# Modulation sums in 1024-wide products, and spread softmax factors behind the value products

## The chip, the cores and the metric

The kernel runs on one core of one Trainium2 chip. The time is the device time of one execution in microseconds (us), as the median of the runs shown.

## What is computed

Two blocks run one after the other on 512 latent tokens of width 1024, with 256 context tokens beside them in the first block, all in float32.

The first block has two layers. Each makes twelve modulation vectors (six for the latent, six for the context) from a condition, projects the normed tokens, runs two attentions of 8 heads (one banded with a sink logit, one dense), merges them under gates, and ends in a gated FFN:

```python
mod   = silu(c) @ w_ada[l] + b_ada[l]          # 6 x 1024 numbers for the latent
mod_c = silu(c_ctx) @ w_ada[l] + b_ada[l]      # 6 x 1024 for the context
h  = rms_norm(x) * (1 + sc1) + sh1
qa, ka, va, qb, kb, vb, ga, gb = split(h @ w_in[l])
ya = window_attention(rope(qa), rope(ka), va, kac, vac, sink)   # p = softmax(s), y = p @ v
yb = full_attention(rope(norm(qb)), rope(norm(kb)), vb, kbc, vbc)
x = x + gt1 * ((sigmoid(ga) * (ya @ w_pa) + sigmoid(gb) * (yb @ w_pb)) @ w_o)
h2 = rms_norm(x) * (1 + sc2) + sh2
x = x + gt2 * swiglu(h2)
```

The second block has a mixer of three attention branches (compressed, selected, windowed), a gated linear recurrence, and a merge of the same form.

## The kernel before, in words

Tokens lie on the free axis and features on the partitions. Every matmul in float32 is three matmuls with both operands split into a high and a low part (`mm3`, L278 to 281). Weights stream through a ring: SyncE loads 128x1024 units (`w`), ScalarE casts the high part (`ws`, L167), GpSimd subtracts for the low part (L171). Each engine works through its own instructions in the order in which the program issues them; the program is one fixed order, written out by hand with hooks at chosen steps.

**Modulation.** Of layer 0 the first 16 weight tiles (shift and scale of the first norm) go through TensorE. The other 80 (`ADB`) are row tiles `wa` of 128x1024: `ada_rows` (L373) multiplies a tile with the broadcast condition `crs` on VectorE and sums along the free axis, for two conditions `c` and, before the change, in two halves of 512 (L382); the elementwise product goes to a tile `junk` that nobody reads. `ada_step` does a whole tile, `ada_half` one condition. `ada_load` issues the tile's load from ScalarE's queue into a ring of two buffers. Steps stand in the query-A projection (`project`, L894, for k = 2 to 7), the query-B projection (k = 0 to 4), the merge of layer 0 (L598, iterations 2 to 11, one condition each), the output projection (`out_proj`, as long as `ada_i < NADA0`) and the FFN of layer 0.

**Projections.** `project` runs over eight k; for each, hooks, then a step, then `mm3` for six token tiles into six PSUM banks (`zs`, `zt`). In query A the hooks carry the keys' work: transposes `ktp`, casts `kTh` on VectorE and ScalarE, low parts `kTl` on GpSimd (`k_parts`, L764 to 775). After it `q_evac` copies each bank to `q`, by turns on VectorE (L318) and ScalarE (L321), two token tiles in one `q` tile; query B's first matmuls reuse the banks.

**Attention.** `Attn.head` works through eight heads of a job (128 queries): scores `sc`, their maximum `nm` on VectorE, the exponential `pb` on ScalarE; three heads later `back` transposes `pb` (`tp`) and the copies go to `PT`. After head 7 `scales` makes the reciprocal sums and spreads them over 512 columns on VectorE (`two` or `Rs`, L1465). One head later `pv` runs: `spread` transposes these factors on TensorE (`Rb`, L1488, four transposes into a bank of the two-bank ring that `tp` uses too), ScalarE copies them back (L1489), the value products go to `pv` (L1477), and `y` multiplies both on VectorE (L1051; in the second block L1828 to 1831). For the last job of an attention (`flush`) the order was products first; for all others `spread` first. The compressed branch (`cmp_ops`, L1890) has its own products `cpv` and calls `spread` behind them. Between heads `Filler` pieces (`fil`) of the merge gates' matmuls are issued.

Of the kernel before, what the change touches and what calls it, by code (L numbers as in the profile page):

```python
# [11 lines left out]
F32 = mybir.dt.float32  # L12
F32R = mybir.dt.float32r
BF16 = mybir.dt.bfloat16
I32 = mybir.dt.int32
AF = mybir.ActivationFunctionType
ALU = mybir.AluOpType
# [4 lines left out]
P = 128  # L22
# [191 lines left out]
class Kern:  # L214
# [158 lines left out]
    def ada_rows(self, i, wt, cs=(0, 1)):  # L373

        V = self.V
        l, e = ADB[i]
        j = e % 4
        if j == 0 and 0 in cs:
            self.ada_sum = self.sm.tile([P, 2, 4, 2], F32, tag="adas", name="adas")
        for c in cs:  # L380
            for h in range(2):
                V.scalar_tensor_tensor(self.junk, wt[:, h * 512:(h + 1) * 512], 1.0, self.crs[:, c, h * 512:(h + 1) * 512],  # L382
                                       op0=ALU.mult, op1=ALU.mult, accum_out=self.ada_sum[:, h, j, c:c + 1])
        if j == 3 and 1 in cs:
            o = self.mods[l][:, e - 3:e + 1, :]
            V.tensor_tensor(o, self.ada_sum[:, 0], self.ada_sum[:, 1], op=ALU.add)
            V.tensor_tensor(o, o, self.C("b_ada", l * 48 + e - 3, 4)[:, :, None].to_broadcast([P, 4, 2]), op=ALU.add)
            self.ada_gain(l, e - 3, 4)

    def ada_open(self, first=False):  # L390

        kp = self.pool(self.right, "kp", 1, side="right")
        self.crs = kp.tile([P, 2, 1024], F32, name="crs")
        self.junk = None if first else kp.tile([P, 512], F32, name="junk")
        self.nc.sync.dma_start(self.crs, self.crow.to_broadcast([P, 2, 1024]))

    def ada_silu(self):
# [156 lines left out]
    def merge(self, pool, l, chunks, ya, yb, gd, nsg, fl):  # L554

        V, S, G, W = self.V, self.S, self.G, self.W
        order = [(n, t0, w) for n in range(8) for (t0, w) in chunks]
        sgs = {}

        def load(i):  # L560
            if i < len(order):
                n, t0, w = order[i]
                sg = pool.tile([P, 2, w], F32, tag=f"sg{w}", name="sg", bufs=nsg)
                for b in range(2):
                    self.nc.sync.dma_start(sg[:, b, :], gd[n][b][:, t0:t0 + w])
                sgs[i] = sg

        ahead = (nsg - 1) * len(chunks)
        for i in range(ahead):
            load(i)  # L570
        def sigmoid(i):
            if i < len(order):
                S.activation(sgs[i], sgs[i], AF.Sigmoid)

        fl.rest()
        low = None
        sigmoid(0)
        for i, (n, t0, w) in enumerate(order):
            if i % len(chunks) == 0:
                W.open(("mp", l, n))  # L580
            sigmoid(i + 1)
            sg = sgs.pop(i)
            for b, y in ((0, ya), (1, yb)) if l < 2 else ((1, yb), (0, ya)):
                pp = self.bank()
                parts = [y(k, t0, w) for k in range(4)]
                for j in range(len(parts[0])):
                    for k in range(4):
                        c0, cw, ab = parts[k][j]
                        self.mm3(pp[:, c0:c0 + cw], W.at(("mp", l, n), (b * 4 + k) * 128), ab, k == 0, k == 3)
                V.tensor_tensor(sg[:, b, :], sg[:, b, :], pp[:, :w], op=ALU.mult)  # L590
            if low:
                low()
            V.tensor_tensor(sg[:, 0, :], sg[:, 0, :], sg[:, 1, :], op=ALU.add)
            hi, lo = self.H(n, t0, w)
            S.copy(hi, sg[:, 0, :])
            if l == 0 and i == 1:
                self.ada_silu()
            elif l == 0 and 1 < i < 12:  # L598
                self.ada_half(i % 2)

            def low(i=i, hi=hi, lo=lo, sg=sg):
                V.tensor_tensor(lo, sg[:, 0, :], hi, op=ALU.subtract)
                load(i + ahead)

        low()
# [181 lines left out]
    def layer(self, l, hooks_in):  # L787
        V, S, G, T, W, C, sm = self.V, self.S, self.G, self.T, self.W, self.C, self.sm
# [88 lines left out]
        def project(c, tiles, free, hooks=()):  # L877
            hk = {}
            for at, fn in hooks:
                hk.setdefault(at, []).append(fn)  # L880
            z = {}
            for i in range(0, min(4, len(tiles)), 2):
                if len(tiles) - i >= 2 and tiles[i] < 4:
                    s = self.psS.tile([P, 2, 512], F32, tag="S", name="zs")
                    z[tiles[i]], z[tiles[i + 1]] = s[:, 0, :], s[:, 1, :]
            for t in tiles:
                if t not in z:
                    z[t] = self.psT.tile([P, 512], F32, tag="T", name="zt")
            for k in range(KD):
                for fn in hk.get(k, ()):  # L890
                    fn()
                if free:
                    W.open(("qkv", l, c), k * 512)
                if l == 0 and (c == "qb" and k < 5 or c == "qa" and k > 1):  # L894
                    self.ada_step(1 if c == "qb" and k == 4 else 2)
                for i, t in enumerate(tiles):
                    if i == len(tiles) // 2:
                        for fn in hk.get(k + 0.5, ()):
                            fn()
                    self.mm3(z[t], self.H(k, t * P, P), W.at(("qkv", l, c), k * 512, 512), k == 0, k == KD - 1)  # L900
            return z
# [25 lines left out]
        if l == 0:  # L927
            project0(hooks_in + [(9, tables)])
        else:
            z = project("kv", lat, False, hooks_in + [(7, tables)])  # L930
            for t in lat:
                kv_copy(t, z[t])
            z = project("kv", ctxt, True, [(2 * t, lambda t=t: kv_rest(t)) for t in lat])
            for t in ctxt:
                kv_copy(t, z[t])
# [10 lines left out]
        pq = self.pool(es, "pq", 1)  # L946
        at = Attn(self, pq, 3)
        if l == 0:
            self.junk = pq.tile([P, 512], F32, tag="qst", name="junk", bufs=2)

        def k_norm():
            self.rsq(rk.rearrange("p a b -> p (a b)"), ssk.rearrange("p a b -> p (a b)"), 12, 1.0 / HD, "kq")
# [51 lines left out]
        if l == 0:  # L1004
            khooks.append((1, self.ada_silu))
        z = project("qa", qt, True, [(0.5, k_norm)] + khooks)
        for t in qt:
            q_evac(0, t, z[t])
        first = dict(q=qs[0, 0])
# [326 lines left out]
class Attn:  # L1336
# [99 lines left out]
    def back(self):  # L1436
        K = self.K
        job, h, pb = self.pend.popleft()
        nb = job["nk"] // P
        for b0 in range(0, nb, 4):  # L1440
            m = min(4, nb - b0)
            tp = K.psT.tile([P, 4, P], F32, tag="T", name="tp")
            for i in range(m):
                K.T.transpose(tp[:, i, :], pb[:, (b0 + i) * P:(b0 + i + 1) * P], K.ident)  # L1444
            K.evac(self.PT[:, b0:b0 + m, h, :], tp[:, :m, :])
        if h == 7:
            rb = self.scales(job)
            self.tail.append((self.n + 1, lambda **kw: self.pv(job, rb, **kw)))

    def scales(self, job):  # L1450
        K = self.K
# [14 lines left out]
                      rs.rearrange("p (g j) -> p j g", g=2)[:, :, :, None].to_broadcast([P, 4, 2, HD]))  # L1466
        return rb

    def pv(self, job, rb, wait=False):
        K = self.K  # L1470
        pv = K.psV.tile([P, 512], F32, tag="V", name="pv")
        nb = job["nk"] // P
        if not wait:
            self.spread(job, rb)
        for b in range(nb):
            for g in range(2):
                K.T.matmul(pv[64 * g:64 * g + 64, :], job["v"](b)[:, 64 * g:64 * g + 64],  # L1477
                           self.PT[:, b, 4 * g:4 * g + 4, :], start=(b == 0), stop=(b == nb - 1))
        if wait:
            self.spread(job, rb)  # L1480
        job["y"](pv, job["Rs"])

    def spread(self, job, rb):
# [9 lines left out]
    def flush(self):  # L1493
        while self.pend:
            self.back()
        while self.tail:
            self.tail.popleft()[1](wait=True)


def second(K, nh):  # L1500
# [324 lines left out]
    def y(tb):  # L1825
        def f(pv, r):
            if parts[tb]:
                V.tensor_tensor(r, pv, r, op=ALU.mult)  # L1828
                V.tensor_tensor(yflat[tb], yflat[tb], r, op=ALU.add)
            else:  # L1830
                V.tensor_tensor(yflat[tb], pv, r, op=ALU.mult)
            parts[tb] += 1
            if parts[tb] == 3:
                V.tensor_tensor(yA[:, tb], yA[:, tb], ga[:, :, tb * P:(tb + 1) * P], op=ALU.mult)
        return f
# [296 lines left out]
```

## Time and profile before

| | |
|---|---|
| median of 3 runs | 2389.41 us (2389.12 to 2389.66) |
| profiled execution, own time | 2386.33 us |
| its span | 2384.30 us |
| mean granted clock of TensorE | 0.991 of full speed |
| TensorE matmuls busy | 97% of the span |
| VectorE busy | 57% |
| ScalarE busy | 37% |
| GpSimd busy | 33% |

The durations below are those of the profiled execution. In the profile PE is TensorE, PEld its weight loads, DVE is VectorE, ACT is ScalarE, POOL is GpSimd and SP is SyncE; L382 is line 382 of the kernel. An entry in square brackets at a row's end is the idle time of its engine ahead of it, and what ended it. Matmuls are pipelined: a duration of 0.39 us can go with starts 0.23 us apart.

### The profile page before, as it was taken

The numbers are of one execution on the slowest core, as the hardware profiler recorded it, in microseconds if no ns is written. First come the engines' busy times: TensorE is split into PE (matmuls) and PEld (weight loads), VectorE is DVE, ScalarE is ACT, GpSimd is POOL, SyncE is SP. The second block draws the span as 40 slices with busy tenths as digits, with TensorE's granted clock in tenths as the row PEclk, the third lists the DMA queues.
The fourth block names the chain that finished last, engine by engine and source line by source line (L and its number), as shares of the span: only waits on it lengthen the run. The fifth ranks groups of instructions, "written<-read, shape, count | busy, mean of one in ns | idle before, by whom it ended". The sixth has DMA issues, their size and how long they took to land.

```text
span 2384.3 us, 33287 instructions
## 1 busy us (share of the span) xinstructions
PE 2305.5 (97%) x13104; PEld 1902.5 (80%) x13104; DVE 1364.8 (57%) x2685; ACT 886.5 (37%) x1606; POOL 793.2 (33%) x367
## 2 busy tenths in 40 slices
PE   8799999999999999999999999999999999999999
PEld 7577787898888888888777777988888888776777
DVE  6976655578577686861685754461111168466552
ACT  4235455542321211122335555432222243464551
POOL 1621222231232333332262322524344433533232
PEclk9999999999999999999999999999999999999999
DMA  7431111363244343432121112513222323432143
GB/s 280 143 124 46 47 56 38 136 221 133 71 131 135 127 152 118 143 99 83 67 80 54 63 45 90 199 57 107 89 97 88 98 80 120 142 120 72 66 159 106
DMA packets 86404, 255.12 MB, mean 107 GB/s; under 512 B 9240, under 2 KB 16928, under 8 KB 85992
## 3 DMA queue, kind: packets, MB, share of 16 engines
q1 hardware_dynamic: 74664, 211.02, 26.1%
q10 hardware_dynamic: 11520, 41.95, 5.3%
q8 instruction: 103, 1.69, 0.3%
q14 instruction: 53, 0.43, 0.1%
q0 software_dynamic: 64, 0.02, 0.0%
HBM read 231.96 MB, written 23.61 MB: 107 GB/s over the span
## 4 chain that ended last, share of the span: by engine, by line
PE 78%; DVE 15%; ACT 3%; issue 2%; DMA 1%; POOL 0%; SPq 0%; ACTq 0%; DVEq 0%; POOLq 0%
PE gup L280 8%; PE gup L281 8%; PE gup L279 8%; PE pv L1477 4%; PE bt L279 4%; PE bt L280 4%; PE bt L281 4%; DVE junk L382 4%; PE tp L1444 4%; PE fil L279 3%; PE fil L281 3%; PE fil L280 3%; PE bs L279 3%; PE bs L281 3%; PE bs L280 3%
## 5 line engine op out<-in xcount | busy, mean ns | idle before, releaser
L171 POOL TENSOR_TENSOR ws<-w,ws 128x1024 fp32r<-128x1024 f32 x273 | 677.2, 2492 | 1313.1 <-ACT ws L167 1263.8
L167 ACT CAST ws<-w 128x1024 fp32r<-128x1024 f32 x274 | 281.0, 1044 | 253.2 <-PE bs L281 67.4
L382 DVE SCALAR_TENSOR_TENSOR junk<-wa,crs 128x512 f32<-128x512 f32 x320 | 344.6, 1077 | 10.8 <-DMA wa<-in_wada_dram 1.8
L280 PE MATMUL gup<-hl,ws 128*128 128x512 f32 (+1 forms) x736 | 284.0, 386 | 1.0 <-DVE hl L297 1.0
L279 PE MATMUL gup<-hl,ws 128*128 128x512 f32 (+1 forms) x736 | 283.6, 385 | 0.0
L281 PE MATMUL gup<-hl,ws 128*128 128x512 f32 (+1 forms) x736 | 283.4, 385 | 0.0
L671 DVE TENSOR_TENSOR g<-g,gup 128x512 f32<-128x512 f32 (+1 forms) x68 | 39.8, 585 | 334.0 <-ACT g L670 334.0
L670 ACT ACTIVATE g<-gup 128x512 f32<-128x512 f32 (+1 forms) x68 | 35.1, 516 | 402.6 <-PE gup L281 402.6
L1424 ACT ACTIVATE pb<-sc,nm 128x768 f32<-128x768 f32 (+3 forms) x160 | 120.5, 753 | 160.3 <-DVE nm L1421 75.4
L280 PEld LDWEIGHTS gup<-hl,ws 128*128 128x128 f32 x736 | 138.3, 188 | 31.6 <-DVE hl L297 2.1
L281 PEld LDWEIGHTS gup<-hl,ws 128*128 128x128 f32 x736 | 138.3, 188 | 30.1
L279 PEld LDWEIGHTS gup<-hl,ws 128*128 128x128 f32 x736 | 138.4, 188 | 29.2
L279 PE MATMUL fil<-hl,ws 128*128 128x512 f32 x384 | 154.6, 403 | 4.8 <-DVE gst L318 4.8
L281 PE MATMUL fil<-hl,ws 128*128 128x512 f32 x384 | 152.0, 396 | 0.1
L280 PE MATMUL fil<-hl,ws 128*128 128x512 f32 x384 | 151.7, 395 | 0.0
L1421 DVE TENSOR_REDUCE nm<-sc 128x1 f32<-128x768 f32 (+3 forms) x160 | 122.7, 767 | 47.5 <-PE sc L1410 46.6
L1444 PEld LDWEIGHTS tp<-cst,pb 128*128 128x128 f32 x896 | 105.8, 140 | 43.5 <-issue 20.1
L1444 PE MATMUL tp<-cst,pb 128*128 128x128 f32 x896 | 137.1, 275 | 3.2 <-ACT PT L321 1.3
L321 ACT COPY PT<-tp 128x512 f32<-128x512 f32 (+3 forms) x210 | 97.7, 476 | 85.7 <-PE tp L1444 85.5
L1376 POOL TENSOR_TENSOR qst<-two,qst 64x512 fp32r<-64x512 f32 x36 | 48.2, 1340 | 195.9 <-DVE qst L1375 189.6
L1409 PE MATMUL sc<-kTh,qst 128*128 128x256 f32 (+2 forms) x288 | 108.2, 376 | 4.3 <-ACT pb L1424 4.2
L279 PE MATMUL bt<-act,ws 128*128 128x512 f32 (+1 forms) x280 | 105.2, 376 | 1.2 <-DVE x L610 1.1
(438 smaller groups left out, 5619.8 us busy)
## 6 DMA issues: line engine op xcount, KB each, us to landing
w<-in_wts_dram SPq DMA_DIRECT2D x274, 512.0 KB, 3.3
wa<-in_wada_dram ACTq DMA_DIRECT2D x80, 512.0 KB, 3.4
gd<-gst SPq DMA_DIRECT2D x48, 256.0 KB, 2.0
sg<-gd SPq DMA_DIRECT2D x48, 256.0 KB, 4.0
wa<-in_wada_dram SPq DMA_DIRECT2D x16, 512.0 KB, 9.9
x<-in_xin_dram SPq DMA_DIRECT2D x8, 384.0 KB, 6.2
zd<-ud SPq DMA_DIRECT2D x1, 2560.0 KB
x<-in_xin_dram SPq DMA_DIRECT2D x4, 512.0 KB, 6.5
```

The lines of the kernel that those rows point to most:

```text
L167: nc.scalar.copy(s[:, 0, :], w)
L171: eng.tensor_tensor(s[:, 1, :], w, s[:, 0, :], op=ALU.subtract)
L279: T.matmul(out, a[0], b[0], start=first, stop=False)
L280: T.matmul(out, a[0], b[1], start=False, stop=False)
L281: T.matmul(out, a[1], b[0], start=False, stop=last)
L321: self.S.copy(dst, src)
L382: V.scalar_tensor_tensor(self.junk, wt[:, h * 512:(h + 1) * 512], 1.0, self.crs[:, c, h * 512:(h + 1) * 512], op0=ALU.mult, op1=ALU.mult, ...
L1409: T.matmul(ps[:, o:o + n], q, job["kh"](g)[:, c0:c0 + n], start=True, stop=False)
L1421: V.tensor_reduce(nm, sc, axis=AX.X, op=ALU.max, negate=True)
L1424: S.activation(pb[:, :nk], sc, AF.Exp, bias=nm, scale=sign, accum_out=job["sums"][:, h:h + 1])
L1444: K.T.transpose(tp[:, i, :], pb[:, (b0 + i) * P:(b0 + i + 1) * P], K.ident)
L1477: K.T.matmul(pv[64 * g:64 * g + 64, :], job["v"](b)[:, 64 * g:64 * g + 64], self.PT[:, b, 4 * g:4 * g + 4, :], start=(b == 0), stop=(b == ...
```

## The change

The sums take one product of 1024 per condition, and the addition of the two halves goes. `junk` is 1024 wide: in float32 where it shares a ring with the query tiles, and in bf16 in the tile that the merge and the FFN of layer 0 use. In the query-A projection steps stand at k = 2, 3 and 4 only; in the merge of layer 0 they go on to iteration 15; as the steps are taken in one sequence, the output projection takes one more (nine for eight). `pv` issues `spread` behind the value products in all jobs.

```diff
-            self.ada_sum = self.sm.tile([P, 2, 4, 2], F32, tag="adas", name="adas")
+            self.ada_sum = self.sm.tile([P, 4, 2], F32, tag="adas", name="adas")
         for c in cs:
-            for h in range(2):
-                V.scalar_tensor_tensor(self.junk, wt[:, h * 512:(h + 1) * 512], 1.0, self.crs[:, c, h * 512:(h + 1) * 512],
-                                       op0=ALU.mult, op1=ALU.mult, accum_out=self.ada_sum[:, h, j, c:c + 1])
+            V.scalar_tensor_tensor(self.junk, wt, 1.0, self.crs[:, c, :], op0=ALU.mult, op1=ALU.mult,
+                                   accum_out=self.ada_sum[:, j, c:c + 1])
         if j == 3 and 1 in cs:
-            o = self.mods[l][:, e - 3:e + 1, :]
-            V.tensor_tensor(o, self.ada_sum[:, 0], self.ada_sum[:, 1], op=ALU.add)
-            V.tensor_tensor(o, o, self.C("b_ada", l * 48 + e - 3, 4)[:, :, None].to_broadcast([P, 4, 2]), op=ALU.add)
+            V.tensor_tensor(self.mods[l][:, e - 3:e + 1, :], self.ada_sum,
+                            self.C("b_ada", l * 48 + e - 3, 4)[:, :, None].to_broadcast([P, 4, 2]), op=ALU.add)
...
-        self.junk = None if first else kp.tile([P, 512], F32, name="junk")
+        self.junk = None if first else kp.tile([P, 1024], BF16, name="junk")
...
-            elif l == 0 and 1 < i < 12:
+            elif l == 0 and i > 1:
                 self.ada_half(i % 2)
...
-                if l == 0 and (c == "qb" and k < 5 or c == "qa" and k > 1):
+                if l == 0 and (c == "qb" and k < 5 or c == "qa" and 1 < k < 5):
                     self.ada_step(1 if c == "qb" and k == 4 else 2)
...
-            self.junk = pq.tile([P, 512], F32, tag="qst", name="junk", bufs=2)
+            self.junk = pq.tile([P, 1024], F32, tag="qst", name="junk", bufs=2)
...
-    def pv(self, job, rb, wait=False):
+    def pv(self, job, rb):
...
-        if not wait:
-            self.spread(job, rb)
         for b in range(nb):
             for g in range(2):
                 K.T.matmul(pv[64 * g:64 * g + 64, :], job["v"](b)[:, 64 * g:64 * g + 64],
                            self.PT[:, b, 4 * g:4 * g + 4, :], start=(b == 0), stop=(b == nb - 1))
-        if wait:
-            self.spread(job, rb)
+        self.spread(job, rb)
         job["y"](pv, job["Rs"])
```

## Rows read from the trace of the kernel before

**Rows 1.** The page, busy time of each engine and share of the span.
```profile
PE 2305.5 (97%) x13104; PEld 1902.5 (80%) x13104; DVE 1364.8 (57%) x2685; ACT 886.5 (37%) x1606; POOL 793.2 (33%) x367
```
**Rows 2.** Waits of TensorE: waiting line, releaser, us in total, times, longest.
```profile
PE zs L279 <- ACT q L321: 17.1, 2, 16.7
PE Rb L1488 <- DVE two L1465: 6.8, 5, 2.5
PE Rb L1488 <- DVE Rs L1465: 1.8, 1, 1.8
```
**Rows 3.** Timeline of TensorE between query A and B: start, us, what.
```profile
104.87 0.39 PE L280 MATMUL zt<-ws,hc 128*128 128x512 f32 x1
105.10 0.40 PE L281 MATMUL zt<-ws,hc 128*128 128x512 f32 x1
122.16 0.79 PE L279 MATMUL zs<-ws,hl 128*128 128x512 f32 x1 [16.66 <-ACT q L321]
```
**Rows 4.** Timeline of VectorE and ScalarE in query A.
```profile
83.35 0.68 DVE L382 SCALAR_TENSOR_TENSOR junk<-wa,crs 128x512 f32<-128x512 f32 x1
...
84.07 1.67 DVE L382 SCALAR_TENSOR_TENSOR junk<-wa,crs 128x512 f32<-128x512 f32 x1
...
87.48 2.77 DVE L382 SCALAR_TENSOR_TENSOR junk<-wa,crs 128x512 f32<-128x512 f32 x1
...
96.13 1.11 DVE L382 SCALAR_TENSOR_TENSOR junk<-wa,crs 128x512 f32<-128x512 f32 x1
...
120.81 0.68 DVE L318 COPY q<-zs 128x512 f32<-128x512 f32 x1
121.52 0.58 ACT L321 COPY q<-zs 128x512 f32<-128x512 f32 x1 [11.43 <-DVE q L318]
```
**Rows 5.** Timeline of VectorE in the merge: a 1024-wide operation with two inputs.
```profile
459.36 1.21 DVE L285 TENSOR_TENSOR yl<-y,yh 128x1024 fp32r<-128x1024 f32 x1
```
**Rows 6.** The products alone in a window: length, VectorE busy, clock, DMA, GB/s.
```profile
83.00:120.85 37.85, 31.49 (x48) 0.83 0.33 111
```
**Rows 7.** Timeline of GpSimd in query A.
```profile
77.05 2.40 POOL L171 TENSOR_TENSOR ws<-w,ws 128x1024 fp32r<-128x1024 f32 x1 [6.73 <-ACT ws L167]
83.51 3.38 POOL L774 TENSOR_TENSOR kTl<-kraw,kTh 64x512 fp32r<-64x512 f32 x2 [4.05 <-DVE kTh L772]
```
**Rows 8.** Windows: length; PE, PEld, DVE, ACT, POOL busy; clock, DMA, GB/s.
```profile
122.10:125.20 3.10, 3.04 (x7) 2.46 (x8) 2.57 (x4) 2.03 (x4) 0.91 (x1) 0.51 0.53 169
518.00:532.00 14.00, 14.00 (x98) 12.94 (x97) 5.78 (x12) 7.03 (x10) 5.04 (x3) 1.00 0.48 163
```
**Rows 9.** Timeline of TensorE: three of the six factor transposes that waited.
```profile
191.75 0.63 PE L1488 MATMUL Rb<-cst,two 128*128 128x128 f32 x4 [2.27 <-DVE two L1465]
...
290.27 0.63 PE L1488 MATMUL Rb<-cst,two 128*128 128x128 f32 x4 [1.38 <-DVE two L1465]
...
1289.12 1.09 PE L1488 MATMUL Rb<-cst,two 128*128 128x128 f32 x4 [2.52 <-DVE two L1465]
```
**Rows 10.** Timeline: value products after two of these, and an evacuation ahead.
```profile
192.30 3.65 PE L1477 MATMUL pv<-PT,vt 128*64 128x512 f32 x16
...
1287.37 0.59 ACT L321 COPY PT<-tp 128x512 f32<-128x512 f32 x1
...
1290.14 4.80 PE L1477 MATMUL pv<-PT,vt 128*64 128x512 f32 x16
```
**Rows 11.** Timeline behind the compressed branch's products in the second block.
```profile
2144.21 0.66 PE L1488 MATMUL Rb<-cst,Rs 128*128 128x128 f32 x4
...
2145.54 0.66 PE L1361 MATMUL qtp<-cst,qtok 128*128 128x128 f32 x4 [0.39 <-ACT Rs L1489]
2145.57 0.69 DVE L1831 TENSOR_TENSOR yA<-cpv,Rs 128x512 f32<-128x512 f32 x1 [3.30 <-issue]
```
**Rows 12.** GpSimd's low parts of keys: count, duration ns min/median/max, starts, forms.
```profile
L774 POOL TENSOR_TENSOR kTl<-kraw,kTh x32: 716/1175/1737, 83.5 to 1239.7; 64x512 fp32r<-64x512 f32 x16, 64x256 fp32r<-64x256 f32 x16
L774 POOL TENSOR_TENSOR k2l<-kraw,k2h x8: 1264/1293/1455, 2046.9 to 2059.0; 64x512 fp32r<-64x512 f32 x8
```

More of the change, by code (lines that the diff above doesn't have):

```diff
@@ L1447, in back @@
             rb = self.scales(job)
-            self.tail.append((self.n + 1, lambda **kw: self.pv(job, rb, **kw)))
+            self.tail.append((self.n + 1, lambda: self.pv(job, rb)))
     def scales(self, job):
@@ L1496, in flush @@
         while self.tail:
-            self.tail.popleft()[1](wait=True)
+            self.tail.popleft()[1]()
 def second(K, nh):
```

## The prediction

> **What bounds the kernel now.** I read the page's engine totals first: TensorE is busy for 2305.5 of 2384.3 us [rows 1], so time can only come from its 79 us of idleness, or from matmuls at the low clock. Then the waits of TensorE, longest in total first: one wait of 16.7 us ends on a ScalarE copy of `q`, and six waits of 8.6 us together end on the softmax factors [rows 2]. No other row there reaches 7 us. The timeline around the long one shows where it lies: the last matmul of the query-A projection starts at 105.10, and the first of query B at 122.16 [rows 3]. The reader is to see that the ScalarE copy named as releaser is not the cause. VectorE's rows say what is: it makes the first copy of the projection's result at 120.81, 15 us after the result was there, because that copy stands in VectorE's own order behind 24 modulation products issued for k = 2 to 7; ScalarE's copy into the same `q` tile follows at 121.52 and TensorE starts 0.06 us after it ends [rows 3, 4]. So VectorE sets the time of this stage and TensorE that of all others.
>
> **Change, part 1: the products.** One weight tile and condition now cost one product of 1024 and one accumulator read instead of two of each. Undisturbed, a 512 product and its read take 0.72 us from start to start (83.35 to 84.07). A two-input VectorE operation of 1024 elements takes 1.21 us (`yl`); with the same 0.04 us between, I take 1.25 for the wide product [rows 4, 5]. The trace has no wide product with an accumulator and a bf16 output; bounds are 1.25 and 2 x 0.72 = 1.44.
>
> In query A, three steps stay (k = 2, 3, 4): 6 wide products for 24 narrow ones. From 83.35 to 120.81 VectorE needs 37.5 us; 31.5 of it are the products and reads [rows 4, 6]. Alone these would take 24 x 0.72 = 17.3. The other 6.0 us are casts, copies and small sums; one of the casts was stalled behind a weight subtraction, 2.1 by the price that follows, so own work is 17.3 + 3.9 = 21.2 and stalls are 16.3. The stalls have a pattern: a product that starts beside GpSimd's 64x512 subtractions takes 1.67 instead of 0.68 (+0.98), beside a 64x256 one 1.11 (+0.42), beside the 128x1024 weight subtraction 2.77 (+2.09) [rows 4, 7]. After the change own work is 6 x 1.25 + 3.5 = 11.0 (the small sums go with step four). GpSimd's queue is unchanged. Taking turns with it, the six products wait 0, 0.98, 2.09, 0.98, 0.42, 0.42 = 4.9; the seven casts of k behind the first, which mostly slipped through before, now meet GpSimd: four at 0.98, two at 0.42, one at 2.09 = 6.9. VectorE ends at 83.35 + 11.0 + 11.8 = 106.2 instead of 120.81. TensorE starts 1.35 us after that (120.81 to 122.16), at 107.5; its last matmul ends at 105.5 (105.10 + 0.40). A gap of 2.0 us stays, and of 16.7 **14.7 are gained**; I take 14.5, as the last copies round up.
>
> The clock: after the gap seven matmuls run at a granted clock of 0.51, the lower of its levels (1.2 GHz), and take 0.43 apart where 0.23 is usual, 1.4 us in all [rows 8]. Gaps of 2.3 and 2.5 us elsewhere were followed by the low clock in one case (1289.12) and not in the other (191.75) [rows 9, 10]. I count nothing, bounds 0 and 1.4 gained.
>
> **Part 2: where the steps go.** Merge iterations 12 to 15 take two of the three steps, four wide products of 1.25 = 5.0 us; the output projection takes the third. Each also brings its load of 512 KB, issued from ScalarE behind the cast of `hi`; that cast waits for a VectorE sum which stands behind the last use of the buffer, so the load finds it free, and in query A three load issues go that stood in ScalarE's order waiting for VectorE. Behind the products in VectorE's order stand the merge's own low halves, for which the output projection waits. From 518 to 532 VectorE is busy for 5.78 of 14 us while TensorE is busy for all 14 [rows 8]: 5.0 us fit, I take 0, and 5.0 if the cover were gone. Everywhere else in layer 0 (query B, merge, output projection, the first FFN) a step costs 2.5 us instead of 2.9; TensorE has no wait there that a product ends, so 0.
>
> **Part 3: the factors.** The four transposes of the spread factors (`Rb`) now follow the value products, in 25 jobs (20 of the layers and 8 of the second block, less the last of each attention, which already ran so). TensorE's six waits, 6.8 + 1.8 = 8.6 us [rows 2], lie ahead of these transposes. With the products first, what is late next is the last evacuation of probabilities (`PT`): in the wait that ends at 1289.12, TensorE was free at 1286.6 and that copy ends at 1287.96, so 1.4 of its 2.52 us stay [rows 9, 10]; the other five I count as gone. 7.2 us go. The wait at 1289.12 also brought the low clock: transposes 1.09 for 0.63, products 4.80 for 3.65 [rows 9, 10], 1.6 us. The shorter wait of 1.38 at 290.27 is followed by transposes at full speed (0.63), so I count these 1.6: gain 8.8.
>
> What is added: the transposes' PSUM bank was emptied by ScalarE beside the products; now that copy has only the next head's transposes over it. The nearest row is the compressed branch, which already runs in this order: its transposes start at 2144.21, the bank is free again at 2145.54, 1.33 later, and TensorE waited 0.39 there [rows 11]. Four factor transposes and the four of the next head cover about 1.05 of it, so 0.3 us in the 12 jobs whose successor has 5 or 6 key blocks (two banks per head), and 0.1 in the other 13: 3.6 + 1.3 = 4.9. Bounds 0 and 25 x 0.8 = 20. Queued behind the waiting multiplication `y` on VectorE are the next evacuation and the next score maximum; it now starts 1.36 after the first factor transpose (2144.21 to 2145.57) [rows 11] instead of at the end of the products. Net of part 3: 8.8 - 4.9 = 3.9 gained.
>
> **Sum.** 14.5 + 3.9 = 18.4 us less. The profiled execution took 2386.33 (span 2384.30), so 2367.9; the median of the runs shown is 3.1 above it, 2389.41, which gives **2371.0 us**.
>
> A rule that speaks against part 1: the Trainium skill, "SBUF — State Buffer", section "SBUF: two separate sides", says that VectorE with two SBUF inputs and GpSimd take a shared port as an exclusive lock for a whole instruction, and the loser blocks fully. The stalls of 0.98 and 2.09 agree with it; no row shows how turns are given when both wait. If GpSimd always came first, it gives the rival "GpSimd first" below.
>
> **Rivals.**
> *GpSimd first.* Fewer VectorE instructions need not mean less waiting, if GpSimd's whole queue passes ahead. Alone its work before VectorE's last cast is 8 x 1.29 + 4 x 0.72 + 3 x 2.40 = 20.4 us [rows 7, 12]; with 11.0 of VectorE it ends at 114.8, TensorE starts at 116.1, and 6.1 are gained: 2389.4 - 6.1 - 3.9 = 2379.4. For it: the stalled cast and products. Against: products now reach their turn after one GpSimd operation, not several.
> *Gap closed.* VectorE keeps up, TensorE runs through and the low clock goes too: 16.7 + 1.4 + 3.9 = 22.0, 2367.4. For it: in the last k of query A six results are finished one after the other, three matmuls 0.23 apart each [rows 3], so the first two are there some 3 us before the last and could be copied in that time. Against: it wants VectorE's stalls at half of what I walked through.
> *Not what it says.* Something else holds query B (weights, the order of `q` copies), and only part 3 counts: 2385.5. Against: its first weights are ready, since TensorE starts at once when the copies end.
> *Slower.* The late `y` blocks VectorE's order and the whole 1.36 us passes to TensorE in each of 25 jobs, 34 us; it decides from (14.5 + 8.8) / 25 = 0.93 us per job. At 1.36 the time is 2389.4 - 23.3 + 34 = 2400.1. Against: in the compressed branch only 0.39 of it reached TensorE, and filler matmuls stand one head later.
>
> **Numbers.** Forecast 0.48, gap closed 0.20, GpSimd first 0.17, not what it says 0.09, slower 0.06. The range 2364 to 2384 takes in the bounds of products and clock, and leaves out the last two; the forecast's own is 2366 to 2377. Within 0.2% (4.8 us, about what a measurement of this kernel tells from no change) lies "not what it says": 0.09. Faster 0.85, slower 0.06.
>
> **What would show it.** TensorE's wait on the `q` copy falls from 16.7 us to 0 to 4; VectorE's first copy of the query-A result comes at about 106; six wide products near 1.2 us when undisturbed. TensorE's waits on the spread factors vanish, and short ones on ScalarE's `Rb` copy, about 0.3 each, appear. Between 518 and 532 TensorE stays fully busy. I am wrong if the first query-B matmul comes later than 114, or if the new waits after the products sum to more than 10 us.

## The result, and where the time went

The changed kernel takes **2347.05 us** (median of four runs, 2345.97 to 2348.39), the kernel before 2389.53 beside it (2389.12 to 2392.06): a ratio of 0.9826 with a 95% interval of 0.9814 to 0.9838. That is 42 us less where 18.4 were forecast. The direction was right, the size less than half, and the time lies 17 us below the range. An effect is given below as a difference of such ratios times 2389 us, because the kernels ran on several chips; by their intervals such a difference is good to some 4 us either way. One execution of the run with `ws` moved, at a granted clock of 0.85, took 2517.6 us and enters no ratio.

The page after, its engine totals (busy us, share of the span, instructions), stands against [rows 1]:

```profile
span 2344.0 us, 32942 instructions
PE 2282.2 (97%) x13104; PEld 1891.3 (81%) x13104; DVE 1319.2 (56%) x2345; ACT 886.8 (38%) x1606; POOL 822.7 (35%) x367
```

TensorE was busy for 79 us less than the span before and for 62 less now: 17 us of idleness went. But its own busy time also fell, by 23 us, at the same 13104 matmuls. No edit changes a matmul; four transposes per job only change places with the value products. This is the part that the prediction has no term for.

The part it had terms for came out nearly as forecast. TensorE's timeline at the end of query A (start, us, what; in brackets the idle time before and what ended it), against [rows 3]:

```profile
105.98 0.40 PE L281 MATMUL zt<-ws,hc 128*128 128x512 f32 x1
106.97 0.50 PE L279 MATMUL zs<-ws,hl 128*128 128x512 f32 x1 [0.59 <-ACT q L321]
```

and VectorE's there, against [rows 4]:

```profile
84.60 1.21 DVE L381 SCALAR_TENSOR_TENSOR junk<-wa,crs 128x1024 f32<-128x1024 f32 x1
...
85.85 2.20 DVE L381 SCALAR_TENSOR_TENSOR junk<-wa,crs 128x1024 f32<-128x1024 f32 x1
...
89.51 3.34 DVE L381 SCALAR_TENSOR_TENSOR junk<-wa,crs 128x1024 f32<-128x1024 f32 x1
...
105.61 0.69 DVE L318 COPY q<-zs 128x512 f32<-128x512 f32 x1
```

Two windows (length; TensorE busy and matmuls; granted clock; DMA share; GB/s): the matmuls behind the boundary, which ran at 0.51 before [rows 8], and the merge's last iterations with the moved products, 16 us earlier than in [rows 8]:

```profile
106.90:110.00 3.10, 3.03 (x13) 1.00 0.56 170
500.00:514.00 14.00, 14.00 (x99) 1.00 0.61 202
```

TensorE's waits that answer to [rows 2]; `Rb` is in none of its waits any more:

```profile
PE tp L1442 <- ACT two L1484: 4.1, 16, 0.6
PE zs L279 <- ACT q L321: 1.0, 2, 0.6
PE tp L1442 <- ACT Rs L1484: 1.2, 4, 0.4
```

Now to the unforecast part. I compared the start of the same-numbered matmul in both traces. After is 16.5 us ahead early in query B and 17.4 in the output projection, then 20 at the start of the first layer's FFN, 29 at its end, 33 at the start of the second layer's FFN and 39 at its end. The second layer's FFN has no product, no moved step, no factor and no gap of TensorE in either kernel; the granted clock is 1.00 in both. So its matmuls themselves come faster. One hundred microseconds of it (length; TensorE busy and matmuls; clock; DMA share; GB/s), in the kernel before and after:

```profile
1650.00:1750.00 100.00, 100.00 (x431) 1.00 0.29 95
```
```profile
1650.00:1750.00 100.00, 100.00 (x439) 1.00 0.29 95
```

The reader is to see that both are 100% busy, so a busy share hides this wholly; only the count of matmuls shows it. From the starts in the trace (mean distance between consecutive matmuls with the same operands and shape, distances over 300 ns left out), a matmul of 512 columns that streams `hl` came every 232.9 ns before and every 229.6 after, one that streams `act` every 233.0 and 229.2. One that streams `ws` against a held `hl` (the projections) came every 232.8 and 233.3: no gain there. (Of a matmul's two operands, the one that streams through, written first in a row, is called the moving one, and the other, loaded ahead of it, the held one.)

What could do this? `ada_sum` shrank from 64 to 32 bytes a partition, in a pool of two buffers that is allocated ahead of nearly everything on the left side of SBUF. In the built programs every tile behind it starts 64 bytes lower: `hl` at byte 39968 of its partition in place of 40032, and `act`, `yh`, `hc`, `q`, `k` and the raw weights likewise. `ws`, on the right, did not move, but for two units in the output projection of each layer, whose buffers lie on the left. Modulo 256, `hl` and `act` went from 96 to 32, and `ws` on the right stayed at 224.

### The profile page after: what moved, and what is told of

The parts are those of the page before. It is cut to its first block, busy times and chain, and to the rows that moved or that the text cites. A ratio compares the mean times of both kernels' runs of the same rounds, so it can differ in the third digit from the quotient of the medians.

```text
span 2344.0 us, 32942 instructions
## 1 busy us (share of the span) xinstructions
PE 2282.2 (97%) x13104; PEld 1891.3 (81%) x13104; DVE 1319.2 (56%) x2345; ACT 886.8 (38%) x1606; POOL 822.7 (35%) x367
## 4 chain that ended last, share of the span: by engine, by line
PE 83%; DVE 11%; ACT 3%; issue 2%; POOL 1%; DMA 1%; SPq 0%; DVEq 0%; ACTq 0%; POOLq 0%
PE gup L280 8%; PE gup L279 8%; PE gup L281 8%; PE bt L279 5%; PE bt L280 5%; PE bt L281 5%; PE pv L1473 4%; PE bs L279 4%; PE bs L280 4%; PE bs L281 4%; PE fil L279 4%; PE tp L1442 4%; PE fil L281 4%; PE fil L280 4%; PE sc L1407 2%; PE sc L1408 2%
## 5 line engine op out<-in xcount | busy, mean ns | idle before, releaser
L171 POOL TENSOR_TENSOR ws<-w,ws 128x1024 fp32r<-128x1024 f32 x273 | 703.5, 2588 | 1256.1 <-ACT ws L167 1193.9
L381 DVE SCALAR_TENSOR_TENSOR junk<-wa,crs 128x1024 bf16<-128x1024 f32 (+1 forms) x160 | 270.5, 1691 | 5.3 <-DMA wa<-in_wada_dram 1.5
L1473 PE MATMUL pv<-PT,vt 128*64 128x512 f32 x448 | 105.7, 599 | 0.4 <-ACT PT L321 0.4
```

The source lines that it names most:

```text
L171: eng.tensor_tensor(s[:, 1, :], w, s[:, 0, :], op=ALU.subtract)
L381: V.scalar_tensor_tensor(self.junk, wt, 1.0, self.crs[:, c, :], op0=ALU.mult, op1=ALU.mult, accum_out=self.ada_sum[:, j, c:c + 1])
```

## Experiments

The theory: the start addresses of TensorE's operands set the distance of its matmuls, and the smaller tile moved them. Rivals: the wide products and their bfloat16 scratch relieve the memory that TensorE reads; or the new order lets TensorE run freer.

**The addresses exchanged.** First the changed kernel with the old addresses:

```diff
-            self.ada_sum = self.sm.tile([P, 4, 2], F32, tag="adas", name="adas")
+            self.ada_sum = self.sm.tile([P, 2, 4, 2], F32, tag="adas", name="adas")[:, 0]
```

> The changed kernel with one thing put back: the tile that takes the sums keeps its old 64 bytes a partition (its second half unused), so every tile allocated behind it on the left (weights, hl, act, yh, q, k) starts 64 bytes higher again, where it started in the kernel before. Every instruction is that of the changed kernel. Theory 1 (the unforecast 22 us come from where the moving operands start, since 512-column matmuls that stream hl, act and yh went from 232.4 to 233.3 ns apart to 228.9 and those that stream ws, whose address did not move, did not): the spacing returns to 232 to 233 ns in the second layer's FFN and the time to about 2369 (2366 to 2372), the query gap staying closed. Theory 2 (the wide products and their bfloat16 scratch take less from the memory that TensorE reads): no change, 2345 to 2349, spacing 228.9. Theory 3 (the new order of factors and moved steps lets TensorE run without short gaps): no change either.

Then the kernel before with the new ones:

```diff
-            self.ada_sum = self.sm.tile([P, 2, 4, 2], F32, tag="adas", name="adas")
+            self.ada_sum = self.sm.tile([P, 2, 4, 2], F32, tag="adas", name="adas", bufs=1)
```

> The kernel before with one thing changed: the tile of the sums is allocated once and not twice, so that every tile behind it on the left starts 64 bytes lower, where it starts in the changed kernel. Products, order of steps and factors are those of before. Theory 1: spacing 228.9 ns wherever hl, act or yh is streamed, and about 22 us less, 2367 (2364 to 2371), with the 16.7 us wait for the query copy still there. Theories 2 and 3: 2389 to 2392, spacing 232 to 233 ns.

Measured: the first 2364.99 us, ratio 0.9912 (0.9898 to 0.9927); the second 2371.67, ratio 0.9935 (0.9918 to 0.9952). The same 100 us of the second layer's FFN, first and second:

```profile
1650.00:1750.00 100.00, 100.00 (x430) 1.00 0.26 90
```
```profile
1650.00:1750.00 100.00, 100.00 (x438) 1.00 0.28 95
```

The counts changed places with the addresses, and the second still has its wait of 16.7 us at query B. Each time lies about 1 us outside the range that the theory gave. Both rivals fall: with every edit in place but the old addresses, TensorE is as slow as before. Of the whole gain 20.5 us (0.9912 less 0.9826) hang on the addresses, and 21.0 (1 less 0.9912) are the edits as written. The second exchange gives 15.5 us for the addresses, which is within the uncertainty of both. The traces agree better: summed over the same-numbered pairs of consecutive matmuls (those at the low clock left out), the old addresses cost 15.9 us in matmuls of 512 columns and 7.2 in those of 256 (5.1 against a second profile of the changed kernel), and the new ones save 15.5 and 5.0 in the kernel before.

**Which starts are quick.** The tile of the sums, allocated once and 32, 96, 192 or 256 bytes wide, put `hl`, `act` and `yh` at 0, 64, 160 and 224 modulo 256. The widest:

```diff
-            self.ada_sum = self.sm.tile([P, 4, 2], F32, tag="adas", name="adas")
+            self.ada_sum = self.sm.tile([P, 8, 4, 2], F32, tag="adas", name="adas", bufs=1)[:, 0]
```

The first two:

> The changed kernel with the tile of the sums allocated once (32 bytes less): hl, act, yh and the weights now start at 0 modulo 128 bytes, where the changed kernel has 32 and the kernel before 96. Theory 1 names no rule yet for which starts are quick: if a row of 1024 bytes is read in aligned pieces, a start at 0 is as quick as 32 or quicker (2335 to 2349); if only the bit for 64 matters, it equals the changed kernel (2345 to 2349). Theories 2 and 3: 2345 to 2349.

> The changed kernel with the tile of the sums allocated once but 96 bytes wide (two thirds of it unused): hl, act, yh and the weights start at 64 modulo 128 bytes. Theory 1: if the bit for 64 decides, spacing 232 to 233 ns and about 2369; if aligned pieces of 64 bytes decide, as quick as a start at 0. Theories 2 and 3: 2345 to 2349.

Measured 2361.55 (0.9896, 0.9882 to 0.9911) and 2371.83 (0.9937, 0.9922 to 0.9952): the first well above all that was expected, the second 3 us above. Both are slow in that FFN (430 matmuls each), though the first starts at a multiple of 256. The addresses of the left side alone have no simple rule. The next run moved the other operand, and the one after it told modulo 128 from modulo 256:

```diff
+        self.rpad = self.pool(ctx, "rp", 1, side="right").tile([P, 16], F32, name="rpad")
         self.W = Stream(
```

> The changed kernel with 64 unused bytes allocated first on the right side, so that the weights' split parts ws (and the pools behind them) start at 32 modulo 128 like hl and act, where they start at 96 in both kernels. ws is the moving operand of the projections (zs, z, zt: 948 matmuls of 512 columns, 233.1 ns apart in the changed kernel) and the held one elsewhere. Theory 1a (the moving operand's own start decides): the projections go to 228.9 ns too, 948 times 4.2 = 4.0 us, 2343 (2340 to 2346), the FFN stays at 228.9. Theory 1b (the start of the moving operand against the held one decides; they are 64 bytes apart where it is quick): with both at 32 the FFN falls back to 233 ns, 2365 to 2369.

> The changed kernel with the tile of the sums allocated once and 192 bytes wide: hl, act and yh start at 160 modulo 256, that is again at 32 modulo 128. If the start modulo 128 decides: 228.9 ns and 2345 to 2349, as the changed kernel. If it is the start modulo 256: 233 ns and 2362 to 2372, as at 0, 64 and 96. Theories 2 and 3 (edits, not addresses) were already contradicted by the two runs with the address exchanged.

Moving `ws`, and with it the pools behind it on the right, from 224 to 160 gave 2364.92 us (0.9899, 0.9882 to 0.9915): the time of the run with the old addresses, though `hl` and `act` stood where the changed kernel has them. What both slow kernels share is the difference of the two starts, 128. So it is the start of the moving operand against that of the held one that counts; the theory of the moving operand alone, which wanted 2343, falls. The next is a case where time and mechanism part: 2346.2 (0.9823, 0.9809 to 0.9838), the changed kernel's time, but with the slow FFN (here in the kernel with `ws` moved, and in the kernel with `hl` at 160):

```profile
1650.00:1750.00 100.00, 100.00 (x432) 1.00 0.28 93
```
```profile
1650.00:1750.00 100.00, 100.00 (x430) 1.00 0.29 94
```

It won the loss back elsewhere: its projections, where `ws` streams and `hl` is held, came every 229.3 ns, and its 256-column matmuls on `hc` every 114.7 in place of 118.2. Summed over pairs as above, its matmuls of 512 columns lost 13.4 us against the changed kernel and those of 256 gained 11.5. Had I read the time alone, I would have concluded "modulo 128".

The widest tile of the four makes the starts equal:

> The changed kernel with the tile of the sums allocated once and 256 bytes wide: hl, act, yh at 224 modulo 256, the same as ws. The runs so far order by the start of the moving operand less that of the held one, modulo 256: 512 columns took 228.9 ns at 64 alone and 232.7 to 234.3 at 32, 96, 128, 160, 192 and 224; 256 columns took 113 to 115 at 192, 117.4 at 32, 118.2 at 64, 119.4 to 120.4 at 96 and 128. Here the difference is 0 for the FFN and for the projections alike, which no run has had. If 64 alone is quick for 512 columns: 233 ns and 2355 to 2372, the rest set by the 256-column price at 0, which is open. If equal starts are a good case too: 229 ns and 2340 to 2350.

Measured: 2343.57 (0.9817, 0.9803 to 0.9830), and the quickest FFN so far, with the projections quick too:

```profile
1650.00:1750.00 100.00, 100.00 (x443) 1.00 0.30 99
```

Little of this reaches the time: against the changed kernel its matmuls of 512 columns gained 12.2 us, and those of 256 lost 10.2 (on `hc` 119.8 ns for 118.2).

Distances of 512-column matmuls (means over a whole trace), ordered by the start of the moving operand less that of the held one, modulo 256:

| difference | ns apart | from |
|---|---|---|
| 0 | 227.5 to 228.1 | `hl` at 224: streaming `hl`, `act` and `ws` |
| 32 | 233.1 to 233.2 | `hl` at 0 |
| 64 | 229.2 to 229.6 | changed kernel; `hl` at 160: projections |
| 96 | 233.3 to 233.6 | `hl` at 64 |
| 128 | 232.7 to 233.1 | kernel before; old addresses; `ws` moved |
| 160 | 234.3 | `hl` at 64: projections |
| 192 | 233.1 to 233.3 | `hl` at 160; changed kernel: projections |
| 224 | 233.3 | `hl` at 0: projections |

The kernel before holds the same comparison within one stage. In its output projection 24 matmuls begin with the first row and 24 with the second, all streaming `hl`, at 96. The first 24 hold a unit of `ws` at 224, the second a unit on the left, at 96: a difference of 0.

```profile
554.32 0.40 PE L279 MATMUL bt<-hl,ws 128*128 128x512 f32 x1
...
559.91 0.39 PE L279 MATMUL bs<-hl,ws 128*128 128x512 f32 x1
...
565.36 0.39 PE L279 MATMUL bt<-hl,ws 128*128 128x512 f32 x1
```

That is 5.59 us and 5.45 us, 232.9 and 227.1 ns apart. Such units came 226.5 to 228.2 ns apart also where `hl` and they start at 0, 32, 64 or 160. At the lower granted clock (1.2 GHz) the starts cost nothing: 426 to 428 ns in the kernel before, at a difference of 128, and as much in the kernel with equal starts.

**One operand by itself.** In these runs other tiles moved along, the raw weights among them. In the kernel before I moved `hl` alone:

```diff
-        self.hl = self.hp.tile([P, 2, KD, NL], F32R, name="hl")
+        self.hl = self.hp.tile([P, 2 * KD * NL + 64], F32R, name="hl")[:, 48:48 + 2 * KD * NL].rearrange(
+            "p (a k n) -> p a k n", a=2, k=KD)
```

> The kernel before with hl alone moved (192 unused bytes ahead of it and 64 behind, so that nothing else moves against 256): hl starts at 32 modulo 256, everything else, act, yh and the raw weights too, where it was. If the starts of TensorE's two operands decide: matmuls of 512 columns that stream hl go from 232.9 to 229.6 ns apart, those that stream act stay at 233.1, those that stream ws against hl go from 232.8 to 233.3; some 3800 matmuls stream hl, the gain is 10 to 13 us, 2374 to 2381. If it is the raw weights or another tile on the left: no change, 2386 to 2391, and 232.9 ns.

Measured 2374.09 (0.9943, 0.9931 to 0.9956), 13.6 us less by moving one tile by 192 bytes. Matmuls streaming `hl` came every 229.7 ns, those streaming `act` still every 232.5, the projections every 233.3, each within 0.2 ns of the table. Summed over pairs, the 512-column matmuls that stream `hl` save 11.7 us of the 13.6, and its 256-column ones 2.3. Hardly any other matmuls changed (0.5 us on `act`), so it is TensorE's operands that do it, not what other engines read or write. Why the difference counts, no run shows.

**256 columns: not settled.** The same was tried on `hc`, in the changed kernel, with 128 unused bytes on each side:

```diff
-        self.hc = self.hcp.tile([P, 2, KD, NC], F32R, name="hc")
+        self.hc = self.hcp.tile([P, 2 * KD * NC + 64], F32R, name="hc")[:, 32:32 + 2 * KD * NC].rearrange(
+            "p (a k n) -> p a k n", a=2, k=KD)
```

> The changed kernel with hc alone 128 bytes further on (128 unused bytes ahead of it and 128 behind, so that nothing else moves against 256). hc is the moving operand of 256 columns in about 1500 matmuls of the FFN and the fill work (118.2 ns at a difference of 64) and gets the difference 192, at which a run had 113 to 115; held against ws in 192 matmuls of the projections it gets 64 (233.8 to 229.3 ns). If the difference of starts decides: 1500 times 4.5 plus 192 times 4.5, 7.6 us, 2339.5 (2337 to 2342). If the quicker 256-column matmuls of that run had another cause (its own act or yh, the kind of stage): 2345 to 2349.

A miss: 2345.89 (0.9824, 0.9810 to 0.9837), no different from the changed kernel. The projections that hold `hc` did go from 233.7 to 229.7 ns. In the fill work among the attention over half of the 256-column matmuls went from 118 to 113 or 114 ns and the others stayed (a mean of 116.0), but in the FFN they stayed at 117.7, with `hc` and `ws` at the very starts that gave 113.9 in the run with `hl` at 160. To see whether such a mode belongs to the execution, the changed kernel ran once more, unedited:

> The changed kernel once more, for a second profile. If the spacing of 256-column matmuls belongs to the program: 117.8 ns in the first FFN and 117.8 in the last stage again. If it belongs to the execution: some stretches at 113.3 this time. The 512-column matmuls: 229.4 and 228.9 again by either.

117.9 ns in the first FFN and 117.8 in the last stage, where the first profile has 118.1 and 117.8 (its one time was 2351.2). The kernel with narrow products below had 113.3 in that last stage at the same addresses. And in the second layer's merge the matmuls that stream `yh` came every 113.0 ns in the first profile of the changed kernel and every 117.5 in the second. So neither the two starts nor the program fix the mode of 256 columns; what does stays open.

**The edits one by one,** at the changed kernel's addresses. The old order of the factors:

```diff
+        if not wait:
+            self.spread(job, rb)
         for b in range(nb):
...
-        self.spread(job, rb)
+        if wait:
+            self.spread(job, rb)
```

> The changed kernel with the old order of the factors: spread ahead of the value products, behind them only at the flush. Everything else, the addresses too, as in the changed kernel. By the prediction's step 3 the six waits on the factors come back (8.6 us of waits, 8.8 with their low clock) and the new short waits on ScalarE's copies go (5.3 us in the trace): 3 to 4 us slower, 2350 to 2351. Rival: the order is worth nothing because TensorE's lost time only moves: 2346 to 2348. Second rival: all of 8.8 is kept since the short waits are there anyway: 2355 to 2356.

2351.13 (0.9844, 0.9830 to 0.9859): 4.3 us, where the prediction's step had 3.9. The two intervals overlap, so the time alone doesn't show it; the waits do. They are back, 9.0 us for 8.6, and the short ones on ScalarE's copies gone:

```profile
PE Rb L1486 <- DVE two L1463: 7.0, 5, 2.5
...
PE Rb L1486 <- DVE Rs L1463: 2.0, 2, 1.8
```

The steps unmoved, products still wide:

```diff
-            elif l == 0 and i > 1:
+            elif l == 0 and 1 < i < 12:
-                if l == 0 and (c == "qb" and k < 5 or c == "qa" and 1 < k < 5):
+                if l == 0 and (c == "qb" and k < 5 or c == "qa" and k > 1):
```

> The changed kernel with the three steps back in the first query projection (12 products of 1024 more there, none behind the 12th tile of the merge); products stay wide. By the prediction's step 1 VectorE then has 24 wide products of about 1.2 to 1.7 us in the stretch before the query copy, 29 to 41 us where before had 31.5 us of narrow ones: the wait of the second query projection comes back with 14 to 25 us, and the time is 2361 to 2372. Rival: the wide products alone had closed the gap: 2346 to 2349.

2360.63 (0.9883, 0.9866 to 0.9899), 13.6 us slower. The gap is back, only 2.8 us shorter than in [rows 3]: wide products alone don't close it. (The expectation counts 24 wide products there; six steps make 12, which took 22.3 us with their reads, so its 14 to 25 us came near by luck.)

```profile
119.74 0.80 PE L279 MATMUL zs<-ws,hl 128*128 128x512 f32 x1 [13.89 <-ACT q L321]
```

And the products in halves again, the steps moved (with the old scratch, and the tile of the sums once at its old size, so that no start moves):

```diff
-            V.scalar_tensor_tensor(self.junk, wt, 1.0, self.crs[:, c, :], op0=ALU.mult, op1=ALU.mult,
-                                   accum_out=self.ada_sum[:, j, c:c + 1])
+            for h in range(2):
+                V.scalar_tensor_tensor(self.junk, wt[:, h * 512:(h + 1) * 512], 1.0, self.crs[:, c, h * 512:(h + 1) * 512],
+                                       op0=ALU.mult, op1=ALU.mult, accum_out=self.ada_sum[:, h, j, c:c + 1])
...
```

> The changed kernel with the products in two halves of 512 columns again (scratch of the kernel before, two sums added at the end, the tile of the sums allocated once so that no address moves), the three steps staying in the merge and the factors behind the value products. By the prediction's step 1 what is left in the first query projection is 24 narrow products of 0.66 us, 15.7 us of 31.5, so the second projection still waits under 2 us: 2346 to 2350, and the width of the products is worth 0 to 3 us. Rival: the width is needed as well, and the gap or waits in the merge and the output projection come back with 5 us or more: 2352 to 2358.

2356.56 (0.9871, 0.9857 to 0.9884), 10.7 us slower: the rival was right. (Three steps make 12 narrow products, not the 24 of the expectation; they took 16.0 us with their reads, near its 15.7.) Query B waits 2.2 us, and where the FFN's norm waits for VectorE, the last sum of squares comes late:

```profile
109.32 0.50 PE L279 MATMUL zs<-ws,hl 128*128 128x512 f32 x1 [2.19 <-ACT q L321]
...
570.57 1.87 PE L469 MATMUL nst<-onec,acc 128*128 128x1 f32 x8 [4.22 <-DVE acc L453]
```

By the starts of the same-numbered matmul, 2.4 us are lost at query B, 2.6 up to the attention, 5.1 in the output projection and at the norm, and 3.0 in the first FFN. Of the 2.6 a stretch at the low clock near 228 us makes 1.6, and the second profile of the changed kernel has it too, so that is not the products' doing. So the moved work found room in the merge and the output projection because it had been made narrower in time. Undoing the move and undoing the width cost 13.6 and 10.7 us, more than the 16.7 that both gained together (21.0 less 4.3). The times alone don't separate these sums; the traces show why, a gap of 13.9 us without the move and a wait of 4.2 at the norm without the width: each leans on the other.

**The version that the runs point to.** The sums go straight into the modulation tile, so that the tile of sums disappears and `hl`, `act`, `yh` fall to 224, like `ws`; `hc` is moved, as above, to a difference of 192 from `ws`.

```diff
-                                   accum_out=self.ada_sum[:, j, c:c + 1])
+                                   accum_out=self.mods[l][:, e, c:c + 1])
...
```

> The version that the runs point to: the changed kernel with the sums written straight into the modulation tile (no tile of sums, 64 bytes less ahead of hl), so that hl, act and yh start at 224 like ws, and hc 192 bytes further on against them (a difference of 192). At a difference of 0 the 512-column matmuls were 226.7 to 228.1 ns apart, for the projections too, and the run had 2343.6. hc at a difference of 192 gave 113 to 117 ns in place of 119.8 in about 1500 matmuls: 4 to 10 us more, 2334 to 2340. If hc's start is worth nothing: 2342 to 2345. If writing into the modulation tile adds waits on VectorE: above 2346.

2341.82 (0.9805, 0.9791 to 0.9818): the lowest median of all, 5.0 us below the changed kernel by the ratios, whose intervals still touch, so the gain over it isn't shown by the times. It lies between the two ranges of the expectation. The 512-column matmuls are at 227.3 to 228.0 ns and gain 12.7 us against the changed kernel, those of 256 lose 6.2; `hc` gave 117.4 for 119.8, just short of the 113 to 117 that I had hoped for.

## Why the prediction was wrong, step by step

**The step that failed** is the first one: "TensorE is busy for 2305.5 of 2384.3 us, so time can only come from its 79 us of idleness, or from matmuls at the low clock". I took the distance of matmuls as fixed. It was not: 20.5 us came from inside the busy time, also in stages that no named edit reaches. The diff showed the cause, a tile of half the size ahead of all others, and I read it as bookkeeping. The trace of before had what would have warned me: 24 matmuls of the output projection at 227.1 ns beside others at 232.9. Its clock rows did too: the prediction read 0.43 us apart at 1.2 GHz, half of which is 0.21 (an estimate from 427 ns: 213 ns), and [rows 3] hold 0.23 at 2.4 GHz. So by that estimate some 20 ns in each of over 5000 such matmuls stood there unexplained, and the range had nothing for it. The Trainium skill, "TensorE: Matmul & The Clock Gate", section "Back-to-back issue gap", gives N / 2.4 + 2.5 ns for a single gap at the full clock, by which 512 columns would be an estimated 216 ns apart, and about 131 ns for a sustained stream. No stage here came below 226.7 at a granted clock of 1.00, so both differ from what is measured, and the section doesn't tie the distance to an address. The runs do.

**Part 1, the products:** right, a little small. VectorE's first copy came at 105.61 (forecast 106.2), query B started at 106.97 (107.5). That these agree so closely is partly luck: the first product started 1.25 us later than before, at 84.60 (the same matmul came 1.1 us later already at 46.6 us, ahead of any edited step; between executions that point lies from 46.6 to 49.4), and the way from it to the copy took 21.0 us where the walk gave 22.8. The six products beside GpSimd took 12.2 us in all where the walk gave 12.4; the longest was 3.34. The casts between them cost less than the walk had for them. The gap became 0.59 us in place of 2.0, and the seven slow matmuls behind it ran at the full clock, 1.4 us that I had counted as nothing. "GpSimd first" is refuted by the time of the copy; "gap closed" is what happened there, 3.0 us more than my term.

**Part 2, the moved steps:** 0 was measured, with TensorE busy for 14.00 of 14 us in the merge's end. The reason was half told: the run with narrow products shows that the cover is thin and that the width pays for it there.

**Part 3, the factors:** right in its waits. The six waits of 8.6 us went; the new waits on ScalarE's copies sum to 5.3 us (4.9 forecast), the longest 0.6; the run that undoes it puts the net at 4.3 (3.9), with some 4 us of uncertainty. The 1.6 us for the low clock are not shown: in that run the wait of 2.52 us came back, and the transposes behind it took 0.63, the time at the full clock. The forecast slower case, 1.36 us passed on in each job, did not occur.

**The sum:** at the old addresses the edits give 21.0 us; I said 18.4. That is 2368.4 against the kernel before of the forecast (2389.41 x 0.9912), in the range and 2.6 below the 2371.0. The changed kernel's time is not.

## What to carry to other kernels

A busy share near 100% is no floor: count matmuls per 100 us, or read the distance of their starts, and compare it between stages and kernels. An edit that changes the size of an early tile moves the start of every tile behind it on its side; hold the starts when an edit is tested, and set them on purpose when it is done. Look at all widths of matmul then: here the starts that were best for 512 columns were not the best for 256. Where work is both made smaller and moved, test the two apart: here the room for the moved part came from the other edit.

## What the runs showed of the hardware

- 512-column matmuls of four-byte data came 226.7 to 234.3 ns apart at a granted clock of 1.00, ordered by the difference of the starts of moving and held operand modulo 256: quickest at 0, next at 64, slow at the six others tried. At the lower clock they came 427 ns apart, at 128 as at 0.
- 256-column matmuls came in groups near 113, 118 and 120 ns. Neither the starts nor the program fixed which: one stage of the changed kernel had 113.0 in one execution and 117.5 in another.
- A product of 1024 with accumulator takes 1.21 us undisturbed, in float32 as in bfloat16 scratch, and up to 3.5 beside GpSimd:

```profile
L381 DVE SCALAR_TENSOR_TENSOR junk<-wa,crs x160: 1208/1224/3498, 84.6 to 1024.8; 128x1024 bf16<-128x1024 f32 x144, 128x1024 f32<-128x1024 f32 x16
```
